# A decoder block on one core: residual rows loaded later, a small transposition moved ahead of a gate product, two value products set side by side

## The chip, the cores and the metric

The kernel runs on one core of a Trainium2 chip. The metric is the device time of one execution in microseconds (us). Before the change the median of three runs is 1652.53 us (1652.47 to 1653.07); the execution that the profiler recorded took 1651.61 us, of which its span covers 1649.8 us. The engines are named as in the profile: PE (matrix products; PEld is its weight load), DVE (vector), ACT (scalar and activation), POOL (GpSimd) and SP, which here only issues DMA transfers.

## The reference

One layer of a hybrid decoder block, 256 tokens, width 2048, float32 throughout. A combined input projection feeds two branches: gated linear attention (GLA, 4 heads) and forgetting attention (FoX, 8 heads). Both are projected to the model width, merged by sigmoid gates, sent through an output projection and added to the scaled residual before a layer norm. A gated MLP with a causal convolution (hidden width 5632), a second layer norm and a per-layer embedding follow.

```python
mix = token_mixers(x, w_in[i], w_gla_lr[i], b_gla_lr[i], gla_norm_g[i],
                   b_forget[i], w_branch_gla[i], w_branch_fox[i], w_out[i])
x = layer_norm(ALPHA * x + mix, ln1_g[i], ln1_b[i])
ffn = conv_gated_mlp(x, w_gate[i], w_up[i], conv_w[i], conv_b[i], w_down[i])
x = layer_norm(ALPHA * x + ffn, ln2_g[i], ln2_b[i])
x = x + jax.nn.sigmoid(x @ w_ple_gate[i]) * (p[i] @ w_ple_proj[i])
```

Within the FoX branch each head computes logits with a cumulative log-forget bias, a causal softmax in two blocks of 128 queries, and the product with the values:

```python
s = (jnp.einsum('bhqd,bhkd->bhqk', q_i, kh)
     + c_i[..., :, None] - c[..., None, :])
pr = jax.nn.softmax(s, axis=-1)
return jnp.einsum('bhqk,bhkd->bhqd', pr, vh)
```

## The kernel before, in words

All large products are split: each operand is written as a rounded part `hi` and a remainder `lo`, and hi·hi, hi·lo and lo·hi are summed in PSUM. A weight unit is 128 x 2048 numbers and comes as two raw rows `raw<unit>_0` and `raw<unit>_1` of 512 KB each. SP loads a raw row into one of four ring buffers, ACT rounds it to `hi` (L212), DVE subtracts to get `lo` (L217), and PE uses both. A ring buffer is free again when its `lo` is written, so a later raw row waits in SP's queue for a DVE instruction. Each engine works through its own queue in order, and SP's order is the program's own; on the other engines a scheduler sets the order by its estimate of when operands and buffers come free, except where the kernel pins it.

**The gates and the FoX heads.** Generators hold small work that is pulled in between the 128-column units of the q and k projections, one step after each unit. `gates_gen` computes the GLA decay of head h with two 96-row products (`psg`, L579); `fox_columns` (L565) transposes the forget sums `zc` into columns `ct` by two tiny PE instructions (`pct`). `fox_gen` handles the heads one behind the other: `turn(h)` transposes the softmax (`pt`, L645) and ACT copies it to `pts`; `values(h)` multiplies with the values (`po`, L652 and L654), after which ACT and DVE split the result.

**The output projection.** `residual("wo", ...)` calls `x_half` twice, once for each half of 1024 output columns. A half takes eight units 120 to 127 (second half: 128 to 135), called pairs 0 to 7 since each covers a pair of 128-row slices of the contraction; a unit's two raw rows belong to the two slices. Four PSUM banks `wo0_00`, `wo0_01`, `wo0_10`, `wo0_11` collect the half (first digit after the underscore: block of 128 tokens; second: block of 512 columns). In the first half, pairs 1, 2, 4 and 5 use a scheme with seven products instead of eight (`seven`, L354), with prepared sums `full` loaded from DRAM, and four more banks `wo0m0` to `wo0m3`; after pair 5 `joined` folds these four into the residual rows `z1` (DVE, `ju` and `z`, L1101 to L1111). After pair 7 the evacuation `ev` adds the four banks onto `z1` (L1090) and takes statistics (L1093). The second half needs four PSUM banks from the same pool of six: `wo1_00` and `wo1_01` take the place of `wo0m0` and `wo0m2`, `wo1_10` and `wo1_11` that of `wo0_00` and `wo0_01`, so that they are free once DVE's evacuation at L1090 has read these.

The `mid` dictionary of each half names callbacks that run after the work of a pair has been recorded: `mid1(t)` loads residual row block `z1[t]` (1 MB, on SP, L1172), `mid1g(i)` loads the layer norm's gain or offset, broadcast to 128 partitions (1 MB, on POOL's queue, `lnb`, L1138). Preparation runs up to three units ahead, so a callback after pair 2 stands in SP's queue behind the loads of pair 4.

## Time and profile before

| | before |
|---|---|
| median of three runs | 1652.53 us |
| profiled execution | 1651.61 us |
| its span | 1649.8 us |
| PE busy | 1643.6 us (100%) |
| DVE busy | 1233.6 us (75%) |
| ACT busy | 882.2 us (53%) |
| POOL busy | 94.8 us (6%) |

Times in the profile's views count from the start of the span. A timeline row gives the start, the duration, the engine, the source line, the operation, what it writes and reads, and how many were merged (x4); behind it in brackets how long the engine was idle before it, and what ended that. Consecutive PE instructions overlap: a row lasts longer than the distance to the next one's start, and it is this distance that a product costs.

### The profile page before, as it was taken

What the parts mean: (1) busy time and instruction counts of PE and PEld (TensorE: products, weight loads), DVE (VectorE), ACT (ScalarE), POOL (GpSimd) and SP (SyncE); (2) the same over time, 40 slices, a digit from 0 to 9 for tenths busy, and PEclk for the clock granted to TensorE, in tenths of its full rate; (3) what the DMA queues carried; (4) which work ended last, traced back from release to release, by engine and by line L of the source; (5) the groups of instructions that cost most, each with busy time, mean ns of one, the idle gap of its engine ahead of it and who ended that gap; (6) DMA issues with size and microseconds to landing.
All of it is one profiled execution on the core that took longest, in us unless ns stands there. A gap on an engine that the chain in (4) does not pass through costs nothing.

```text
span 1649.8 us, 24319 instructions
## 1 busy us (share of the span) xinstructions
PE 1643.6 (100%) x8956; PEld 1426.9 (86%) x8956; DVE 1233.6 (75%) x1819; ACT 882.2 (53%) x1268; POOL 94.8 (6%) x219
## 2 busy tenths in 40 slices
PE   9999999999999999999999999999999999999998
PEld 8988888888888888888888888888888888888887
DVE  6666658668856667786888778888887688788784
ACT  6745545445555455555565545555455566466643
POOL 0000000000000000000010011111110011010000
PEclk9999999999999999999999999999999999999999
DMA  7765555555555685668747678889886589799354
GB/s 299 233 196 189 168 186 178 183 179 179 174 180 195 242 307 192 193 206 316 267 155 234 232 257 334 316 325 337 322 285 229 192 292 325 270 329 363 141 187 170
DMA packets 107527, 394.23 MB, mean 239 GB/s; under 512 B 12504, under 2 KB 13408, under 8 KB 104464
## 3 DMA queue, kind: packets, MB, share of 16 engines
q1 hardware_dynamic: 97008, 352.62, 62.0%
q0 software_dynamic: 10256, 39.86, 6.3%
q8 instruction: 70, 1.15, 0.3%
q14 instruction: 49, 0.40, 0.1%
q10 hardware_dynamic: 144, 0.20, 0.0%
HBM read 365.36 MB, written 27.27 MB: 238 GB/s over the span
## 4 chain that ended last, share of the span: by engine, by line
PE 96%; DMA 2%; ACT 1%; DVE 1%; issue 0%; SPq 0%; ACTq 0%
PE psu L290 9%; PE psg L290 9%; PE dn L334 7%; PE psm L290 7%; PE gv L334 5%; PE gr L334 5%; PE pg L334 5%; PE psu L292 5%; PE psg L292 5%; PE psm L292 4%; PE psa L290 3%; PE wo L334 3%; PE dn L354 3%; PE fv L496 3%; PE dn0m L354 2%; PE psfq L290 2%
## 5 line engine op out<-in xcount | busy, mean ns | idle before, releaser
L217 DVE TENSOR_TENSOR lo<-raw,hi 128x1024 fp32r<-128x1024 f32 x502 | 611.5, 1224 | 271.9 <-ACT hi L212 270.3
L212 ACT ACTIVATE hi<-raw 128x1024 fp32r<-128x1024 f32 x502 | 528.7, 1059 | 465.4 <-DMA raw<-in_wu_dram 114.6
L290 PE MATMUL psu<-x1T,hi 128*128 128x512 f32 x688 | 236.0, 389 | 0.0
L290 PE MATMUL psg<-x1T,hi 128*128 128x512 f32 x672 | 230.5, 389 | 0.0
L292 PE MATMUL psu<-x1T,lo 128*128 128x256 f32 x688 | 189.9, 276 | 0.0
L292 PE MATMUL psg<-x1T,lo 128*128 128x256 f32 x672 | 185.5, 276 | 0.0
L290 PE MATMUL psm<-xT,hi 128*128 128x512 f32 x512 | 175.5, 390 | 0.0
L290 PEld LDWEIGHTS psu<-x1T,hi 128*128 128x128 f32 x688 | 129.1, 188 | 26.7
L290 PEld LDWEIGHTS psg<-x1T,hi 128*128 128x128 f32 x672 | 126.2, 188 | 26.1
L292 PE MATMUL psm<-xT,lo 128*128 128x256 f32 x512 | 141.4, 276 | 0.0
L292 PEld LDWEIGHTS psu<-x1T,lo 128*128 128x128 f32 x688 | 129.2, 188 | 0.0
L292 PEld LDWEIGHTS psg<-x1T,lo 128*128 128x128 f32 x672 | 126.1, 188 | 0.0
L290 PEld LDWEIGHTS psm<-xT,hi 128*128 128x128 f32 x512 | 96.1, 188 | 19.9
L334 PE MATMUL dn<-hi,hT 128*128 128x512 f32 x352 | 97.8, 389 | 0.0
L292 PEld LDWEIGHTS psm<-xT,lo 128*128 128x128 f32 x512 | 96.2, 188 | 0.2
L290 PE MATMUL psa<-oT,hi 128*128 128x512 f32 x256 | 87.8, 389 | 0.0
L334 PEld LDWEIGHTS dn<-hi,hT 128*128 128x128 f32 x352 | 66.0, 188 | 13.7
L292 PE MATMUL psa<-oT,lo 128*128 128x256 f32 x256 | 70.7, 276 | 0.0
L334 PE MATMUL gr<-hi,xT 128*128 128x512 f32 x256 | 70.6, 392 | 0.0
L334 PE MATMUL gv<-hi,xT 128*128 128x512 f32 x256 | 70.4, 391 | 0.0
L334 PE MATMUL pg<-hi,x2T 128*128 128x512 f32 (+1 forms) x224 | 60.0, 376 | 0.0
L290 PEld LDWEIGHTS psa<-oT,hi 128*128 128x128 f32 x256 | 48.1, 188 | 10.1
(357 smaller groups left out, 3070.4 us busy)
## 6 DMA issues: line engine op xcount, KB each, us to landing
raw<-in_wu_dram SPq DMA_DIRECT2D x528, 512.0 KB, 4.9
comb<-in_wu_dram SPq DMA_DIRECT2D x22, 768.0 KB, 8.9
tsd<-comb POOLq DMA_DIRECT2D x22, 512.0 KB, 7.3
top<-tsd SPq DMA_DIRECT2D x22, 512.0 KB, 5.8
fvraw<-in_wfv_dram SPq DMA_DIRECT2D x15, 524.0 KB, 7.9
rawf<-in_wu_dram SPq DMA_DIRECT2D x14, 512.0 KB, 9.5
top<-in_wu_dram SPq DMA_DIRECT2D x22, 256.0 KB, 6.8
hi<-hsd POOLq DMA_DIRECT2D x22, 256.0 KB, 4.9
```

The source lines that it names most:

```text
L212: c = nc.scalar.activation(hi, raw, AF.Copy, bias=0.0, scale=1.0)
L217: return nc.vector.tensor_tensor(lo, raw, hi.bitcast(F32), ALU.subtract)
L290: nc.tensor.matmul(ps, lhsT=hi[i // 8 if hoff == 0 else 0][:, w0 % 1024:w0 % 1024 + P], rhs=a[:, kt % 4, :], start=first and i == 0, stop= ...
L292: nc.tensor.matmul(ps[:, 256:512], lhsT=lo[i // 8 if hoff == 0 else 0][:, w0 % 1024:w0 % 1024 + P], rhs=a[:, kt % 4, 0:256], start=False, ...
L334: nc.tensor.matmul(bs[j][:, 0:m], lhsT=x, rhs=v[:, o:o + m], start=first and i == 0, stop=last and i == 2)
L354: nc.tensor.matmul(ps, lhsT=a, rhs=v, start=m and first and i == 0, stop=m and last and i == 2)
L496: nc.tensor.matmul(fbk[t][c][:, 0:n], lhsT=x, rhs=w[:, o:o + n], start=kt == 0 and i == 0, stop=kt == 15 and i == 2)
```

## The change

Three edits. The four callbacks of the output projection move: both residual row blocks are now loaded after pair 4 of the first half was recorded (before: after pairs 2 and 3), and the two affine rows after pairs 0 and 2 of the second half (before: after pair 6 of the first and pair 1 of the second). `fox_columns` runs just ahead of the gates of the last GLA head, in the same step, and not in a step of its own behind them. The values of the last FoX head follow those of the head before in the same step, and the loop loses its last round.

```diff
     def gates_gen():
         for h in range(H):
+            if h == H - 1:
+                fox_columns()
             gla_gates(h)
             yield
-        fox_columns()
...
-        for h in range(FH + 1):
-            if h < FH:
-                turn(h)
+        for h in range(FH):
+            turn(h)
             if h + 1 < FH:
                 logits(h + 1)
             if h > 0:
                 values(h - 1)
             if h + 1 < FH:
                 softmax(h + 1)
+            else:
+                values(h)
             yield
             yield
...
-    residual("wo", mT, 16, z1, st1, ({2: lambda: mid1(0), 3: lambda: mid1(1), 6: lambda: mid1g(0)}, {1: lambda: mid1g(1), 3: lambda: (pq.append(ple_prep(0)), mid1x())}), end=end1, ws=WOW)
+    residual("wo", mT, 16, z1, st1, ({4: lambda: (mid1(0), mid1(1))}, {0: lambda: mid1g(0), 2: lambda: mid1g(1), 3: lambda: (pq.append(ple_prep(0)), mid1x())}), end=end1, ws=WOW)
```

How this moves instructions is seen at three places. The first is SP's queue in the middle of the output projection's first half. `raw126` is pair 6, `raw127` pair 7, `raw128` the second half's first pair, `z10` and `z11` are the residual row blocks. Before:

```order
L149 DMA full124_7336<-tfd_105 128x2048
L1172 DMA z10_7247<-in_x_dram 128x2048
L147 DMA rawl125_7377<-in_wu_dram 128x512
L148 DMA raw125_7376<-in_wu_dram 128x1024
L149 DMA full125_7378<-tfd_105 128x2048
L1172 DMA z11_7248<-in_x_dram 128x2048
L205 DMA raw126_0_7421<-in_wu_dram 128x1024
L205 DMA raw126_1_7427<-in_wu_dram 128x1024
L205 DMA raw127_0_7454<-in_wu_dram 128x1024
L205 DMA raw127_1_7460<-in_wu_dram 128x1024
```

Now:

```order
L149 DMA full124_7336<-tfd_105 128x2048
L147 DMA rawl125_7376<-in_wu_dram 128x512
L148 DMA raw125_7375<-in_wu_dram 128x1024
L149 DMA full125_7377<-tfd_105 128x2048
L205 DMA raw126_0_7419<-in_wu_dram 128x1024
L205 DMA raw126_1_7425<-in_wu_dram 128x1024
L1174 DMA z10_7247<-in_x_dram 128x2048
L1174 DMA z11_7248<-in_x_dram 128x2048
L205 DMA raw127_0_7454<-in_wu_dram 128x1024
L205 DMA raw127_1_7460<-in_wu_dram 128x1024
```

Both 1 MB blocks moved behind pair 6's raw rows; pair 7's raw rows have the same transfers ahead of them as before. POOL's order, with the two affine rows, and what each of these two waits for are the same in both kernels.

The second place is PE at the start of the second half of the output projection. Before, the first 23 products of the half all go into `wo1_00` and `wo1_01`, from both slices of pairs 0 and 1, and only then comes the other token block, with the wait for its bank. The last three of the 23 and what follows:

```order
L334 MATMUL wo1_00_7579<-lo129_1_7544,mT0_5909 128x512 [waits DVE_49]
L334 MATMUL wo1_01_7580<-lo129_1_7544,mT0_5909 128x512
L334 MATMUL wo1_00_7579<-hi129_1_7543,mT0_5909 128x512
L334 MATMUL wo1_10_7581<-hi128_0_7499,mT0_5909 128x512 [waits DVE_49]
L334 MATMUL wo1_10_7581<-lo128_0_7500,mT0_5909 128x512
L334 MATMUL wo1_10_7581<-hi128_0_7499,mT0_5909 128x512
L334 MATMUL wo1_11_7582<-hi128_0_7499,mT0_5909 128x512 [waits DVE_49]
```

Now, from the half's first product on:

```order
L334 MATMUL wo1_00_7577<-hi128_0_7499,mT0_5909 128x512 [waits DVE_49,Activation_49]
L334 MATMUL wo1_01_7578<-hi128_0_7499,mT0_5909 128x512 [waits DVE_49]
L334 MATMUL wo1_00_7577<-lo128_0_7500,mT0_5909 128x512
L334 MATMUL wo1_01_7578<-lo128_0_7500,mT0_5909 128x512
L334 MATMUL wo1_00_7577<-hi128_0_7499,mT0_5909 128x512
L334 MATMUL wo1_01_7578<-hi128_0_7499,mT0_5909 128x512
L334 MATMUL wo1_10_7579<-hi128_0_7499,mT0_5909 128x512 [waits DVE_49]
L334 MATMUL wo1_11_7580<-hi128_0_7499,mT0_5909 128x512 [waits DVE_49]
```

The first use of `wo1_10` has moved from the 24th place of the half to the 7th. In both kernels it waits for the same DVE instruction, the evacuation of `wo0_00` (L1090 before, L1092 now), and `wo1_11` for that of `wo0_01`; DVE's own order there is the same in both: the `lo` of pair 7, then `joined` mixed with the `lo` of units 128 and 129, then the evacuation.

The third place is PE where the last FoX head is turned. Before:

```order
L292 MATMUL psk0_2067<-xT3_109,lo24_1_1942 128x256
L645 MATMUL pt7_2103<-ident_82,lg_1990 128x128 [waits DVE_49,Activation_49]
L645 MATMUL pt7_2103<-ident_82,lg_1990 128x128 x2
L652 MATMUL po6_2109<-pts_1985,fv_120 128x256
L654 MATMUL po6_2109<-pts_1985,fv_120 128x128
L290 MATMUL psk1_2126<-xT0_106,hi25_0_2009 128x512
```

Now:

```order
L292 MATMUL psk0_2067<-xT3_109,lo24_1_1942 128x256
L646 MATMUL pt7_2103<-ident_82,lg_1990 128x128 [waits DVE_49,Activation_49]
L646 MATMUL pt7_2103<-ident_82,lg_1990 128x128 x2
L653 MATMUL po6_2109<-pts_1985,fv_120 128x256
L655 MATMUL po6_2109<-pts_1985,fv_120 128x128
L653 MATMUL po7_2114<-pts_2107,fv_120 128x256 [waits Activation_49]
L655 MATMUL po7_2114<-pts_2107,fv_120 128x128
L290 MATMUL psk1_2131<-xT0_106,hi25_0_2009 128x512
```

`po7` reads `pts_2107`, ACT's copy of `pt7`. Before, it stood 64 products (two units) further on, behind the units `psk1` and `psk2`; now two products lie between `pt7` and it. The small transposition `pct` also moved on PE, from its place one unit behind the last gate product `psg` to directly ahead of it.

## The prediction

> **What bounds the kernel now.** I read the page's engine line first, then PE's waits, then the timelines of the places where the edits fall.

> ```profile
> PE 1643.6 (100%) x8956; PEld 1426.9 (86%) x8956; DVE 1233.6 (75%) x1819; ACT 882.2 (53%) x1268; POOL 94.8 (6%) x219
> PE warm_ps L128 <- DVE warm L125: 1.2, 1, 1.2
> PE wo L334 <- DVE lo L217: 0.2, 1, 0.2
> PE ptl L1056 <- DVE x1T L878: 0.2, 1, 0.2
> ```

> PE is never out of work: in 1649.8 us it waits twice after the start, for 0.2 us each. So no transfer and no other engine can give more than tenths of a microsecond back, while anything that makes PE wait is paid in full. One of the two waits, in the output projection (`wo`), lies where the residual loads move.

> **The loads: what can be gained.** SP's queue, the DMA issues of the stretch 761 to 766 us against those of the whole run, ACT, and PE around pair 6:

> ```profile
> 755.97 0.42 SPq L1172 DMA_DIRECT2D z<-in_x_dram  x1
> 760.46 0.43 SPq L1172 DMA_DIRECT2D z<-in_x_dram  x1
> raw<-in_wu_dram SPq DMA_DIRECT2D x2, 512.0 KB, 17.2
> raw<-in_wu_dram SPq DMA_DIRECT2D x528, 512.0 KB, 4.9
> 777.44 1.06 ACT L212 ACTIVATE hi<-raw 128x1024 fp32r<-128x1024 f32 x1 [5.75 <-DMA raw<-in_wu_dram]
> 780.20 1.06 ACT L212 ACTIVATE hi<-raw 128x1024 fp32r<-128x1024 f32 x1 [1.70 <-DMA raw<-in_wu_dram]
> 778.96 0.84 PE L334 MATMUL wo<-hi,mT 128*128 128x512 f32 x3
> 782.57 0.73 PE L334 MATMUL wo<-lo,mT 128*128 128x512 f32 x2 [0.21 <-DVE lo L217]
> 789.96 1.07 PE L334 MATMUL wo<-hi,mT 128*128 128x512 f32 x4
> 791.32 0.39 PE L334 MATMUL wo<-hi,mT 128*128 128x512 f32 x1
> ```

> Pair 6's raw rows, queued behind both residual blocks, take 17.2 us to land where 4.9 is usual; the second reaches ACT at 780.20 and PE has to wait for its `lo`. From 789.96 to 791.32 PE issues four products and two of the next row: 1.36 / 6 = 0.227 us each, the undisturbed rate. Pair 6 starts at 778.96; the first two of the four at 789.96 end pair 7, so 46 products lie between, which would take 10.43 us and took 11.00. The wait with its surroundings costs **0.57 us**. With the blocks behind pair 6's rows, 2 MB fewer stand ahead of these, 5 us at the 415 GB/s below; they land several microseconds sooner and the 0.57 is gained: the second half then starts at 790.41 (two products after 789.96) less 0.57, **789.84**.

> **The loads: what is late next.** The second half's seventh product, now the first on `wo1_10`, waits for DVE's evacuation of `wo0_00`. DVE in this stretch (rows left out are more of `joined` and `lo`), and PE where this product stood before:

> ```profile
> 778.53 1.23 DVE L217 TENSOR_TENSOR lo<-raw,hi 128x1024 fp32r<-128x1024 f32 x1 [5.40 <-ACT hi L212]
> 781.29 3.67 DVE L217 TENSOR_TENSOR lo<-raw,hi 128x1024 fp32r<-128x1024 f32 x3 [1.54 <-ACT hi L212]
> 784.88 0.68 DVE L1106 TENSOR_TENSOR ju<-ju,wo0m 128x512 f32<-128x512 f32 x1
> 785.48 0.68 DVE L1111 SCALAR_TENSOR_TENSOR z<-z,wo0m 128x512 f32<-128x512 f32 x1
> ...
> 790.56 1.23 DVE L217 TENSOR_TENSOR lo<-raw,hi 128x1024 fp32r<-128x1024 f32 x1 [0.33 <-ACT hi L212]
> ...
> 793.50 1.22 DVE L217 TENSOR_TENSOR lo<-raw,hi 128x1024 fp32r<-128x1024 f32 x1
> 794.64 1.28 DVE L1090 TENSOR_TENSOR z<-z,wo 128x512 f32<-128x512 f32 x2
> 795.41 0.62 PE L334 MATMUL wo<-hi,mT 128*128 128x512 f32 x2
> ```

> The evacuation starts at 794.64; one such operation takes 0.68 (row at 784.88) and the next starts 0.60 later, so `wo0_00` is free at 795.32 and `wo0_01` at 795.92. Before, PE got there with its 24th product, the second of the row at 795.41, at 795.64: 0.3 us after the bank was free, with nothing lost. Now it gets there at 789.84 + 6 x 0.227 = **791.20**.

> Can DVE be sooner? Twelve instructions stand between the `lo` of pair 7 and the evacuation, and DVE works through them in 9.8 us (784.88 to 794.64) with one gap of 0.33. They begin when pair 7's second `lo` is written, which hangs on this landing:

> ```profile
> 782.65 1.06 ACT L212 ACTIVATE hi<-raw 128x1024 fp32r<-128x1024 f32 x1 [0.18 <-DMA raw<-in_wu_dram]
> 755.00:760.00 5.00, 5.00 (x24) 4.14 (x23) 5.00 (x8) 2.60 (x5) 0.00 (x0) 1.00 0.73 224
> 760.00:765.00 5.00, 5.00 (x24) 4.14 (x23) 2.97 (x4) 2.83 (x3) 0.00 (x0) 1.00 1.01 415
> 775.00:780.00 5.00, 5.00 (x24) 4.02 (x23) 1.23 (x1) 1.06 (x1) 0.00 (x0) 1.00 1.00 413
> ```

> ACT's rounding of that row waits for the DMA until 782.65. From 760 to 780 the DMA engines are full (shares 1.01 and 1.00 in the first and last of four windows). Pair 7's rows keep the same bytes ahead of them as before, the two affine rows on POOL's queue included, so reordering what is ahead does not let them land sooner. They might land later, if taking the block issued at 755.97 out of the not yet full stretch (0.73) leaves the engines idle; the `full` load issued just ahead of it, at 1 MB, has 2.5 us of work for them, so I expect little, up to 1 us. What can fall away is the gap of 0.33 before 790.56, where DVE waits, by way of ACT, for a raw row of the second half: with pair 6 done early, the rows ahead of that one are issued sooner and it shares the DMA engines with fewer.

> From DVE's end to PE's start it takes 0.05: the first `lo` of the row at 781.29, 1.23 long, ends at 782.52, and PE, which waited for it, goes on at 782.57. So PE has the bank between 795.0 and 795.4. PE waits 3.75 to 4.2 us at `wo1_10`, issues one product, and waits 0.60 - 0.23 = 0.37 more at `wo1_11`: 4.1 to 4.55 lost. Behind the waiting product stands everything PE has left to do. Less the 0.57, the edit costs **3.5 to 4.0; I take 3.85**, nearer the end with DVE unchanged, because a restart after a wait costs some 0.1 too (the row at 782.57: 0.73 for two where 0.62 is usual). With pair 7 later by 1 us it is 4.9; with the banks freed 1 us sooner 2.8. Nothing later gives it back, since PE finds no other wait to shorten but 0.2 at `ptl`. The affine rows keep their place and their releasers on POOL: 0.

> **The values.** PE and ACT where the last head is turned:

> ```profile
> 202.94 0.60 PE L652 MATMUL po<-pts,fv 128*128 128x256 f32 x2
> 203.37 0.38 PE L654 MATMUL po<-pts,fv 128*128 128x128 f32 x2
> 203.51 0.47 PE L290 MATMUL psk<-xT,hi 128*128 128x512 f32 x1
> 202.74 1.06 ACT L212 ACTIVATE hi<-raw 128x1024 fp32r<-128x1024 f32 x1 [1.66 <-PE psk L290]
> 203.97 0.48 ACT L116 ACTIVATE pts<-pt 128x384 f32<-128x384 f32 x1
> ```

> `po7` now follows `po6` and could issue at about 203.50. It needs `pts`, which ACT writes from 203.97 to 204.45, because a rounding of 1.06 us that itself waited for PE stands first in its queue. Before, two units of other products covered this copy; the cover is gone. PE waits 204.45 + 0.05 - 203.50 = **1.0 us**, and behind it waits the whole unit `psk1`. Bounds: +0.9 if the two seams between `po` and `psk` become one (0.47 on the first `psk` where 0.40 is usual), +1.2 with the 0.1 of a restart. I take 1.0.

> **The transposition.** PE around it:

> ```profile
> 80.42 0.28 PE L292 MATMUL psfq<-xT,lo 128*128 128x256 f32 x1
> 80.62 0.28 PE L565 MATMUL pct<-ident,zc 8*128 8x8 f32 x2
> 80.84 0.50 PE L290 MATMUL psfq<-xT,hi 128*128 128x512 f32 x1
> 81.18 0.28 PE L292 MATMUL psfq<-xT,lo 128*128 128x256 f32 x1
> 61.12 0.28 DVE L560 COPY zc<-zf 8x256 f32<-8x256 f32 x1
> ```

> The interlude takes 81.18 - 80.42 = 0.76 us; the two `psfq` products alone take 0.34 (0.227 for 512 columns, half of it for 256), so it costs 0.42. Its operand `zc` is ready at 61.40, long before. Next to the gate product it has one seam with `psfq` in place of two: it saves 0.2 at best (half of it), and costs 0.1 more at worst if its seam with `psg` is as dear. I take **-0.05**.

> **The sum.** 3.85 + 1.0 - 0.05 = **+4.8 us**: 1651.61 becomes 1656.4 in a profiled execution. The median was 0.92 above the profiled one; the same on top gives **1657.3**. By the terms' own bounds (2.8 to 4.9, 0.9 to 1.2, -0.2 to +0.1) the likeliest case reaches from +3.5 to +6.2, most of it +4.0 to +5.6.

> **The rivals.** (1) *The array's clock drops in the long wait.* The last window of the run shows the granted clock (the column after POOL's) falling when PE stops:

> ```profile
> 1645.00:1650.00 5.00, 0.49 (x5) 0.29 (x3) 1.32 (x4) 0.38 (x1) 0.00 (x0) 0.92 0.29 105
> 1.20 3.25 PE L128 MATMUL warm_ps<-warm 128*128 128x512 bf16 x8 [1.20 <-DVE warm L125]
> ```

> PE ends at 1645.49; a mean of 0.92 with half speed at the end means 0.8 us of it, so the drop came at 1649.2, 3.7 us later. The wait here is 3.75 to 4.2. Were the clock halved for 3.7 us behind it, PE would lose 1.85 of them: +6.65, 1659.2. At the start of the run eight products took 3.25 us, 0.41 each against 0.227, so half speed does occur on a PE that comes from idleness. Against it: the array still works on the last product after its issue (0.39 against a distance of 0.227), and the reaction is seen once, at one phase. [...] Chance 0.10.

> (2) *The bank is free sooner.* If pair 7's rows land 2 us sooner, because the DMA engines move the new order faster, `joined` starts sooner too and the loss at `wo1_10` shrinks to 1.85: the sum is +2.8, 1655.3. For it: DVE stood idle for 5.40 us ahead of 778.53 and would have time for pair 6 there; against it the full DMA windows. Chance 0.13.

> (3) *Not slower.* The same mechanism pushed to its end: the evacuation must be done by 791.2 at the first use, 4.1 us sooner. Only then does the edit gain its 0.57, and the sum is -0.57 + 1.0 - 0.05 = +0.4, 1652.9, no change that can be told. It needs pair 7's rows in at about 778.5, 1.7 MB earlier in a full queue. Chance 0.08.

> (4) *Pair 7's rows are late.* They stand directly behind both blocks now. Landing 1.5 us later would move the evacuation with them and make it +6.3, 1658.8. Chance 0.07.

> That leaves 0.62 for the forecast. A measurement of this kernel tells 0.2%, 3.3 us, from no change, so slower begins at 1655.8. Slower: the forecast, (1), (4) and a little of (2): 0.82; same 0.16; faster 0.02. The range that leaves out about 2 in 10 is 1655.0 to 1659.4.

> **What would show it.** In PE's waits of the changed kernel two new rows: one at `wo` for DVE's `z` (the evacuation) of about 4 us in the second half's first pair, with a second of 0.4, and one at `po` for ACT's `pts` of about 1 us; the old row at `wo` for `lo` gone. ACT's rounding of pair 6 should start some 8 us sooner, that of pair 7's second row near 782.7 on a clock that is set back by the 1.0 from the values. The forecast is wrong if DVE's evacuation starts near 791, if `po7` issues without a wait, or if a window behind the long wait shows a clock below 1.

## The result, and the profile after

The changed kernel takes 1658.66 us, median of 6 runs (1657.33 to 1659.93), against 1652.38 us of the kernel before (6 runs, 1651.65 to 1653.07): the ratio is 1.0038 with a 95% interval of 1.0026 to 1.0049, so it is 6.3 us slower. 1657.3 was predicted, with a range of 1655.0 to 1659.4. The profiled execution is the quickest of the six, 1657.33 us with a span of 1655.6.

The engine line of the changed kernel's profile page:

```profile
PE 1646.2 (99%) x8956; PEld 1428.2 (86%) x8956; DVE 1232.6 (74%) x1819; ACT 881.9 (53%) x1268; POOL 96.4 (6%) x219
```

And two rows of its PE waits (engine, line, what it waited for: us in total, times, longest):

```profile
PE wo L334 <- DVE z L1092: 2.1, 1, 2.1
PE po L653 <- ACT pts L116: 0.7, 1, 0.7
```

Both forecast waits are there, each shorter in these rows than the 4 and 1 us forecast, and the old wait at `wo` for `lo` is gone. PE's timeline of the changed kernel around the long wait, with DVE's evacuation that ends it:

```profile
792.49 0.61 PE L334 MATMUL wo<-hi,mT 128*128 128x512 f32 x2
795.22 1.18 PE L334 MATMUL wo<-hi,mT 128*128 128x512 f32 x2 [2.12 <-DVE z L1092]
796.20 1.05 PE L334 MATMUL wo<-lo,mT 128*128 128x512 f32 x2
797.05 1.91 PE L334 MATMUL wo<-hi,mT 128*128 128x512 f32 x4
794.49 1.27 DVE L1092 TENSOR_TENSOR z<-z,wo 128x512 f32<-128x512 f32 x2
```

Without the wait the first product on `wo1_10` would have issued at 792.49 + 2 x 0.227 = 792.94; it issues at 795.22, so **2.28 us** are lost. The last PE row shows something else: four products in 1.91 us where the row of the kernel before has 1.07. The stretches of the changed kernel, cut where the clock changes (length, then busy time of PE, PEld, DVE, ACT and POOL with instruction counts, then the granted clock, the DMA share and GB/s):

```profile
789.27:792.69 3.42, 3.42 (x16) 2.82 (x16) 3.42 (x5) 1.06 (x1) 0.00 (x0) 1.00 0.81 228
792.69:796.10 3.41, 1.19 (x4) 0.47 (x3) 3.41 (x6) 2.11 (x2) 0.00 (x0) 1.00 0.77 257
796.10:799.51 3.41, 3.41 (x9) 2.65 (x9) 3.41 (x7) 1.06 (x1) 0.00 (x0) 0.50 0.40 139
799.51:802.93 3.42, 3.42 (x16) 2.79 (x16) 3.42 (x4) 1.07 (x1) 0.00 (x0) 1.00 0.35 108
```

**The clock was halved for 3.41 us behind the wait**: 9 products were busy there where the stretches around it have 16, some 1.6 us lost. So the first rival came true although the wait was shorter than the one it had been given a chance of 0.10 for.

The values, PE and ACT of the changed kernel:

```profile
203.32 0.38 PE L655 MATMUL po<-pts,fv 128*128 128x128 f32 x2
204.45 0.70 PE L653 MATMUL po<-pts,fv 128*128 128x256 f32 x2 [0.75 <-ACT pts L116]
205.13 0.47 PE L290 MATMUL psk<-xT,hi 128*128 128x512 f32 x1
202.69 1.06 ACT L212 ACTIVATE hi<-raw 128x1024 fp32r<-128x1024 f32 x1 [1.66 <-PE psk L290]
203.92 0.48 ACT L116 ACTIVATE pts<-pt 128x384 f32<-128x384 f32 x1
```

The bracket counts the idle time from the end of `po6`. By starts it is more: in the kernel before, the next product follows 0.14 us behind the start of such a row (203.37 and 203.51), so `po7` could have issued at 203.46 and did at 204.45, **0.99 us** later.

Where the time went, by the first product of each stage (after less before, one profile each): 0.45 us more before the first `psfq` unit, in waits of `fv` at the start that no edit touches; -0.50 from there to the first `psq`, where the transposition lies; **+1.79** between the first `psk` and `gv` (values); **+3.80** between the first `wo` and `pp` (residual); in the 800 us behind it -0.2 and, in the last stage, +0.4. Tempting as it is, this is no proof of what each edit costs: the experiments show that two of the four numbers depend on other things.

### The profile page after: what moved, and what is told of

Its sections match the earlier page's. It is cut to its first block, busy times and chain, and to the rows that moved or that the text cites. A ratio compares the mean times of both kernels' runs of the same rounds, so it can differ in the third digit from the quotient of the medians.

```text
span 1655.6 us, 24318 instructions
## 1 busy us (share of the span) xinstructions
PE 1646.2 (99%) x8956; PEld 1428.2 (86%) x8956; DVE 1232.6 (74%) x1819; ACT 881.9 (53%) x1268; POOL 96.4 (6%) x219
## 4 chain that ended last, share of the span: by engine, by line
PE 95%; DMA 2%; DVE 1%; ACT 1%; issue 0%; SPq 0%; ACTq 0%; DVEq 0%
PE psu L290 9%; PE psg L290 9%; PE dn L334 7%; PE psm L290 7%; PE gv L334 5%; PE gr L334 5%; PE pg L334 5%; PE psu L292 5%; PE psg L292 5%; PE psm L292 4%; PE psa L290 3%; PE dn L354 3%; PE wo L334 3%; PE fv L496 3%; PE dn0m L354 2%; PE psk L290 2%
## 5 line engine op out<-in xcount | busy, mean ns | idle before, releaser
L217 DVE TENSOR_TENSOR lo<-raw,hi 128x1024 fp32r<-128x1024 f32 x502 | 610.7, 1222 | 284.5 <-ACT hi L212 283.1
L212 ACT ACTIVATE hi<-raw 128x1024 fp32r<-128x1024 f32 x502 | 528.5, 1059 | 474.2 <-DMA raw<-in_wu_dram 110.3
L290 PE MATMUL psu<-x1T,hi 128*128 128x512 f32 x688 | 236.0, 389 | 0.0
L290 PE MATMUL psg<-x1T,hi 128*128 128x512 f32 x672 | 230.5, 389 | 0.0
L292 PE MATMUL psu<-x1T,lo 128*128 128x256 f32 x688 | 189.9, 276 | 0.0
L292 PE MATMUL psg<-x1T,lo 128*128 128x256 f32 x672 | 185.5, 276 | 0.0
L290 PE MATMUL psm<-xT,hi 128*128 128x512 f32 x512 | 175.5, 390 | 0.0
L290 PEld LDWEIGHTS psu<-x1T,hi 128*128 128x128 f32 x688 | 129.2, 188 | 26.7
L290 PEld LDWEIGHTS psg<-x1T,hi 128*128 128x128 f32 x672 | 126.1, 188 | 26.2
L292 PE MATMUL psm<-xT,lo 128*128 128x256 f32 x512 | 141.4, 276 | 0.0
L292 PEld LDWEIGHTS psu<-x1T,lo 128*128 128x128 f32 x688 | 129.1, 188 | 0.0
L292 PEld LDWEIGHTS psg<-x1T,lo 128*128 128x128 f32 x672 | 126.2, 188 | 0.0
L290 PEld LDWEIGHTS psm<-xT,hi 128*128 128x128 f32 x512 | 96.1, 188 | 19.8
L334 PE MATMUL dn<-hi,hT 128*128 128x512 f32 x352 | 97.8, 389 | 0.0
L292 PEld LDWEIGHTS psm<-xT,lo 128*128 128x128 f32 x512 | 96.2, 188 | 0.2
L290 PE MATMUL psa<-oT,hi 128*128 128x512 f32 x256 | 87.8, 389 | 0.0
L334 PEld LDWEIGHTS dn<-hi,hT 128*128 128x128 f32 x352 | 66.0, 188 | 13.7
L292 PE MATMUL psa<-oT,lo 128*128 128x256 f32 x256 | 70.7, 276 | 0.0
L334 PE MATMUL gr<-hi,xT 128*128 128x512 f32 x256 | 70.6, 392 | 0.0
L334 PE MATMUL gv<-hi,xT 128*128 128x512 f32 x256 | 70.3, 391 | 0.0
L334 PE MATMUL pg<-hi,x2T 128*128 128x512 f32 (+1 forms) x224 | 60.0, 376 | 0.0
L334 PE MATMUL wo<-hi,mT 128*128 128x512 f32 x192 | 54.6, 396 | 2.2 <-DVE z L1092 2.1
## 6 DMA issues: line engine op xcount, KB each, us to landing
raw<-in_wu_dram SPq DMA_DIRECT2D x528, 512.0 KB, 4.9
tsd<-comb POOLq DMA_DIRECT2D x22, 512.0 KB, 7.4
top<-tsd SPq DMA_DIRECT2D x22, 512.0 KB, 5.6
rawf<-in_wu_dram SPq DMA_DIRECT2D x14, 512.0 KB, 9.9
```

What stands on the lines that cost most here:

```text
L212: c = nc.scalar.activation(hi, raw, AF.Copy, bias=0.0, scale=1.0)
L217: return nc.vector.tensor_tensor(lo, raw, hi.bitcast(F32), ALU.subtract)
L290: nc.tensor.matmul(ps, lhsT=hi[i // 8 if hoff == 0 else 0][:, w0 % 1024:w0 % 1024 + P], rhs=a[:, kt % 4, :], start=first and i == 0, stop= ...
L292: nc.tensor.matmul(ps[:, 256:512], lhsT=lo[i // 8 if hoff == 0 else 0][:, w0 % 1024:w0 % 1024 + P], rhs=a[:, kt % 4, 0:256], start=False, ...
L334: nc.tensor.matmul(bs[j][:, 0:m], lhsT=x, rhs=v[:, o:o + m], start=first and i == 0, stop=last and i == 2)
```

## The experiments

"Before" is timed on the same chip beside each group (medians 1652.38 for e1 to e4, 1652.33 for e5 to e8, 1652.92 for e9 to e12). The last column is the time from the first product of `wo` to the first of `pp` in the run's profile; the kernel before has 85.29, the changed one 89.10.

| run | what | median us | ratio to before (95%) | `wo` to `pp` |
|---|---|---|---|---|
| e1 | residual part | 1658.64 | 1.0037 (1.0023 to 1.0050) | 91.57 |
| e2 | residual part, products in the old order | 1652.59 | 1.0001 (0.9992 to 1.0010) | 85.57 |
| e3 | transposition part | 1651.94 | 0.9997 (0.9989 to 1.0006) | 85.59 |
| e4 | values part | 1654.71 | 1.0015 (1.0006 to 1.0023) | 84.74 |
| e5 | e1, affine rows late | 1652.35 | 0.9999 (0.9990 to 1.0008) | 84.97 |
| e6 | before, affine rows late | 1652.14 | 0.9997 (0.9988 to 1.0006) | 84.71 |
| e7 | e1, six products more ahead of the wait | 1657.10 | 1.0027 (1.0018 to 1.0036) | 87.19 |
| e8 | whole change, products in the old order | 1653.75 | 1.0007 (0.9998 to 1.0016) | 84.71 |
| e9 | residual blocks alone | 1657.68 | 1.0032 (1.0019 to 1.0044) | 91.66 |
| e10 | values one unit behind | 1652.44 | 0.9999 (0.9990 to 1.0008) | 85.31 |
| e11 | e3, e6 and e10 together | 1651.89 | 0.9995 (0.9986 to 1.0004) | 84.71 |
| e12 | whole change again | 1657.88 | 1.0035 (1.0022 to 1.0048) | 88.48 |

**e1, the residual part alone** (from the kernel before):

```diff
-({2: lambda: mid1(0), 3: lambda: mid1(1), 6: lambda: mid1g(0)}, {1: lambda: mid1g(1), 3: lambda: (pq.append(ple_prep(0)), mid1x())})
+({4: lambda: (mid1(0), mid1(1))}, {0: lambda: mid1g(0), 2: lambda: mid1g(1), 3: lambda: (pq.append(ple_prep(0)), mid1x())})
```

> Only the residual's part of the change: both blocks behind pair 6's raw rows, the affine rows in the second half; transposition and values stay as before. In the changed kernel PE loses 3.80 us between the start of the second half of the output projection and its end. If that part acts alone: 3.5 to 4.1 us slower than before, a wait of about 2 us at `wo` for DVE's `z`, and 3.4 us of halved clock behind it. If the loss needed the other two edits as well (the shift of 1.74 us that they bring before this place sets the wait against the clock's windows in another way): no halved clock, and 1.8 to 2.4 us slower.

It loses 6.26 us, as much as the whole change and more than either expectation. Its row of PE's waits:

```profile
PE wo L334 <- DVE z L1090: 3.7, 1, 3.7
```

Its PE and DVE timelines at that place:

```profile
791.55 0.61 PE L334 MATMUL wo<-hi,mT 128*128 128x512 f32 x2
795.84 1.39 PE L334 MATMUL wo<-hi,mT 128*128 128x512 f32 x2 [3.68 <-DVE z L1090]
795.10 1.28 DVE L1090 TENSOR_TENSOR z<-z,wo 128x512 f32<-128x512 f32 x2
```

And its stretches between changes of the clock, with the columns of above:

```profile
791.54:794.96 3.42, 0.62 (x3) 0.19 (x1) 3.42 (x5) 1.06 (x1) 0.00 (x0) 1.00 0.79 252
794.96:798.37 3.41, 2.53 (x6) 1.83 (x7) 3.41 (x7) 1.06 (x1) 0.00 (x0) 0.50 0.67 217
798.37:801.79 3.42, 3.42 (x10) 2.64 (x9) 3.42 (x5) 1.06 (x1) 0.00 (x0) 0.50 0.04 16
801.79:805.20 3.41, 3.41 (x16) 2.79 (x15) 2.55 (x3) 1.06 (x1) 0.00 (x0) 1.00 0.69 220
```

The wait is 795.84 - 792.00 = 3.84 us, what had been forecast for the whole change, and the clock is halved for twice 3.41 us: in the first of these PE still waits at the start and is busy for 2.53 us, and only after the second, in which PE never stopped (3.42 of 3.42 us), is the clock full again. Lost at half speed: some 14 products at 0.2 us each, 2.8. With the floor of 84.71 in the table's last column, 84.71 + 3.84 + 0.37 + 2.8 = 91.7, and 91.57 was measured.

**e2, the same loads with the products in the old order:**

```diff
-                mm(i, unit(), (0, 1))
+                w = unit()
+                if name == "wo1" and i < 2:
+                    us = [w] if i == 0 else us + [w]
+                    mm(i, w, (0,))
+                    if i == 1:
+                        mm(0, us[0], (1,))
+                        mm(1, us[1], (1,))
+                else:
+                    mm(i, w, (0, 1))
```

> The residual's part again, with the products of the second half's pairs 0 and 1 written so that those on token block 0 of both pairs come first, as they stood before; DMA issues and evacuations are those of e1. If the loss comes from the order of the products alone: `wo1_10` is reached some 24 products after the half starts, 3.9 us later than in e1, by then the bank is free, the waits for `z` and for pair 6's `lo` are both gone, and it is 0.3 to 0.6 us faster than before. If the loss comes from the loads (rows of pair 7 or of the second half landing later): 1 us or more slower, with a wait at `wo` for DVE's `lo` or `z`.

The six microseconds are gone: the loss comes from the order of the products that the moved loads brought about. The expected gain of 0.3 to 0.6 did not come either, and one row of PE's timeline of this run shows where it went:

```profile
796.29 0.74 PE L334 MATMUL wo<-lo,mT 128*128 128x512 f32 x2 [0.52 <-DVE lo L217]
```

DVE works without a gap from 786 to 797 us on `joined`, `lo` and evacuations; the wait at pair 6 has moved to the second half.

**e3, the transposition part, and e4, the values part**, each alone:

```diff
+            if h == H - 1:
+                fox_columns()
             gla_gates(h)
             yield
-        fox_columns()
```

```diff
-        for h in range(FH + 1):
+        for h in range(FH):
...
             if h + 1 < FH:
                 softmax(h + 1)
+            else:
+                values(h)
```

> Only the transposition's part of the change. By the forecast's price (one seam less): 0.05 us faster, between 0.2 faster and 0.1 slower. By the pace theory (PE goes through pairs of unit products at 0.341 or 0.352 us each, and what small product stood last before them decides which): the 70 slow pairs behind the transposition become fast, 0.5 to 0.8 us faster, and the trace shows no slow stretch between 76 and 105 us.

> Only the values' part of the change. By the wait for ACT's copy of `pts` alone: 1.0 us slower (0.9 to 1.2). With the pace theory: 0.7 us of wait, some 0.3 us of seams, and about 80 pairs of unit products behind it at 0.352 in place of 0.341 us, another 0.8: 1.6 to 2.0 us slower, with one slow stretch from 205 to 243 us.

e3's 0.44 us cannot be told from nothing. The `L290` products of the same 22 us behind the transposition in the kernel before (length, PE busy with the count, PEld, clock, DMA share, GB/s):

```profile
82.00:104.00 22.00, 22.00 (x64) 11.79 (x64) 1.00 0.57 190
```

The same stretch of e3 has two more:

```profile
82.00:104.00 22.00, 22.00 (x66) 12.15 (x65) 1.00 0.58 193
```

But so has e1, which does not touch this place:

```profile
82.00:104.00 22.00, 22.00 (x66) 12.18 (x65) 1.00 0.58 193
```

There are two paces, one pair (`hi` and `lo`) each about 0.350 us or each about 0.340 us, and e1 has the quick one without the edit, as have seven of the nine profiles without it. So the -0.50 in the comparison above is not the edit's doing, and my pace theory of e3 falls. What the edit is worth shows among the profiles with the quick pace: from the first `psfq` to the first `psfk` these seven take 45.11 or 45.12 us, and e3, e8, e11 and e12, which have the edit, 45.07 or 45.08. That is 0.04 us less, as forecast. (The changed kernel has 45.20, with a slower first unit ahead of the edit.)

e4 is 2.33 us slower by the medians (by the interval 1.0 to 3.8). In its profile 1.94 us are lost between `psk` and `gv`: the joined group takes 1.10 more than the two apart (2.24 us beyond `pt7` and the products around it, against twice 0.57), and 1.0 of it is the late issue of `po7`. The rest is pace, seen again in a count of `L290` products from 217 to 240 us, here in the kernel before:

```profile
217.00:240.00 23.00, 23.00 (x69) 12.74 (x68) 1.00 0.59 188
```

In e4 there are two fewer:

```profile
217.00:240.00 23.00, 23.00 (x67) 12.39 (x66) 1.00 0.58 190
```

The second profile of the whole change (e12) has as many as before:

```profile
217.00:240.00 23.00, 23.00 (x69) 12.68 (x68) 1.00 0.59 193
```

Behind the joined group the slow pace held in three of four profiles that have it (e4, e8, the changed kernel) and not in e12; behind a `po7` of its own the pace was quick in all profiles (ten). 80 pairs by 0.010 are the missing 0.8 us. What sets the pace is open.

**e5 and e6, the affine rows late on SP's queue**, on top of e1 and of the kernel before (e5's table of loads is that of e1; e6 keeps the blocks at 2 and 3):

```diff
-        q = nc.gpsimd if li == 0 else nc.sync
+        q = nc.sync
```

```diff
-({2: lambda: mid1(0), 3: lambda: mid1(1), 6: lambda: mid1g(0)}, {1: lambda: mid1g(1), 3: lambda: (pq.append(ple_prep(0)), mid1x())})
+({2: lambda: mid1(0), 3: lambda: mid1(1)}, {0: lambda: mid1g(0), 2: lambda: mid1g(1), 3: lambda: (pq.append(ple_prep(0)), mid1x())})
```

> e1 with one change: the two affine rows (1 MB each) go onto SP's queue behind raw rows of the second half, so they no longer share the DMA engines with pair 7's raw rows; the order of the products is that of e1 (`wo1_10` at the seventh place). If DVE's evacuation of `wo0_00` hangs on the bytes ahead of pair 7's second row, that row lands up to 5 us sooner (2 MB at 413 GB/s), the evacuation starts some 4 us sooner, and the wait of 3.7 us at `wo` for `z` with the halved clock is gone: between 0.6 us faster than before and 0.6 slower. If the evacuation is bound by DVE's own work or by when the rows are issued: 4 us or more slower, as in e1.

> The kernel before with that change alone (affine rows on SP's queue in the second half); residual blocks and the order of the products stay as before. Pair 6's rows then share with 2 MB less: the wait of 0.2 us at `wo` for `lo` goes or stays, between 0.6 us faster and no change. If the rows on SP's queue hold up raw rows of the second half: up to 1 us slower, with a wait at `wo` for `lo` near 800 us.

In e5 the order is e1's and the wait is gone. ACT's rounding of pair 7's two rows and DVE's evacuation in e5:

```profile
778.12 1.06 ACT L212 ACTIVATE hi<-raw 128x1024 fp32r<-128x1024 f32 x1 [6.56 <-DMA raw<-in_wu_dram]
779.33 1.06 ACT L212 ACTIVATE hi<-raw 128x1024 fp32r<-128x1024 f32 x1
790.90 1.28 DVE L1090 TENSOR_TENSOR z<-z,wo 128x512 f32<-128x512 f32 x2
```

The same two roundings in e1:

```profile
782.32 1.06 ACT L212 ACTIVATE hi<-raw 128x1024 fp32r<-128x1024 f32 x1 [10.64 <-DMA raw<-in_wu_dram]
783.53 1.06 ACT L212 ACTIVATE hi<-raw 128x1024 fp32r<-128x1024 f32 x1 [0.15 <-DMA raw<-in_wu_dram]
```

Row and evacuation are both 4.2 us sooner, for 2 MB taken out of full DMA engines (in e1 their share is 1.00 to 1.02 from 765 to 780 us): the evacuation does hang on the bytes ahead of pair 7's second row. With that, 0.57 was to be gained, and the profiles show 0.32 and 0.58 of it (84.97 and 84.71 in the last column where the kernel before has 85.29); the timed runs cannot tell it from nothing.

**e7, six products more ahead of the wait:**

```diff
+                if name == "wo1" and i < 1:
+                    mm(i, w, (0,))
+                    mm(i, w, (1,))
```

> e1 with the products of the second half's pair 0 written with all twelve on token block 0 first, so that `wo1_10` is reached six products, 1.36 us, later: a wait of about 2.4 us in place of 3.7. If a wait of that length already halves the clock for 3.4 us (as in the changed kernel, where PE waited 2.1 us): 3.5 to 4.5 us slower than before. If the clock needs an idle stretch as long as its window: no halved clock, 2.0 to 2.6 us slower.

Its median is 4.8 us slower, beyond both expectations, and its eleven times spread from 1653.11 to 1659.91: in the quickest the mean granted clock is 1.000, in four of the others 0.998. Its profile is of an execution in which the clock stayed full. The row of PE's waits:

```profile
PE wo L334 <- DVE z L1095: 1.8, 1, 1.8
```

The two stretches that hold the wait:

```profile
791.12:794.53 3.41, 2.71 (x12) 1.90 (x11) 3.41 (x5) 1.70 (x2) 0.00 (x0) 1.00 0.80 231
794.53:797.94 3.41, 2.21 (x8) 1.61 (x9) 3.41 (x7) 1.31 (x2) 0.00 (x0) 1.00 0.76 251
```

The wait lies across a boundary of the clock's 3.41 us stretches (counted back in steps of 3.413 us from the clock's drop at the end of the run, since it does not change here), and PE is busy 2.71 and 2.21 us in the two. So it also matters how the wait lies in these stretches, as e12 below shows: its wait, across a boundary as well, is longer than the changed kernel's, 3.27 us against 2.28, and leaves the clock full. The size of the median is not explained by this one profile.

**e8, the whole change with the products in e2's order** (its diff is e2's, on the changed kernel):

> The whole change, with the order of products of e2 in the second half (no early `wo1_10`). If the parts only seemed not to add up because the values' delay is swallowed by the long wait at `wo`, then without that wait it shows in full: +2.3 (values) + 0.2 (e2) - 0.4 (transposition), about 2.1 us slower than before. If the values' part costs little once the transposition has moved too: 0 to 1 us slower.

1.42 us slower by the medians, between the two expectations; the interval, 0.9998 to 1.0016, just reaches no change. No wait is left at `wo`. In the profile the values cost 1.78 us (`psk` to `gv`); the stage from `wo` to `pp` is 0.86 shorter than in e2, whose code is the same there. So in these two profiles part of the values' delay is made up in that stage even without the long wait; whether by PE's later arrival or by how the loads happened to land is not shown.

**e9, the residual blocks alone, and e12, the whole change again:**

```diff
-({2: lambda: mid1(0), 3: lambda: mid1(1), 6: lambda: mid1g(0)}, {1: lambda: mid1g(1), 3: lambda: (pq.append(ple_prep(0)), mid1x())})
+({4: lambda: (mid1(0), mid1(1)), 6: lambda: mid1g(0)}, {1: lambda: mid1g(1), 3: lambda: (pq.append(ple_prep(0)), mid1x())})
```

> Half of the residual's part: only the two residual blocks go behind pair 6's raw rows, the affine rows' loads stay where they were written before. The order of the products comes out as in e1 (`wo1_10` seventh). If the blocks' place alone makes that order and the long wait: 5.5 to 6.5 us slower, as e1, with a wait of 2 to 4 us at `wo` for `z` and a halved clock. If the affine rows' place takes part: 1 us or more apart from e1.

> The whole change once more, beside e9 on one chip, for a second profile. If the values' delay (about 1.8 us) is swallowed by the wait at `wo`: its median lies within 0.7 us of e9's, its wait at `wo` for `z` is 1.4 to 2 us shorter than e9's, and the joined values are followed by the slow pace up to the next group. If the wait does not depend on when PE arrives: about 2 us slower than e9.

The blocks alone make the order and the loss. e9 is 4.76 us slower, less than expected and 1.5 less than e1; but the whole change, too, is 4.96 slower here and 6.28 in its first runs, and `wo` to `pp` takes as long in e9 as in e1 (91.66 and 91.57), so this does not speak for a part of the affine rows. And the whole change is 0.2 us from e9, though the values alone cost 2.33: by the medians of five runs each, which spread over 3 to 4 us, the values add nothing. The two profiles do not show how. e9 waits 4.0 us and e12 3.27, but PE arrives at the wait at the same time in both (the last product before it starts at 792.22 and 792.18), and the pace behind e12's joined values was the quick one, so that they cost it only 0.68 us (`psk` to `gv`). The shorter wait comes from an evacuation that starts 0.79 sooner, at 794.94 against 795.73. The row of e12's PE waits:

```profile
PE wo L334 <- DVE z L1092: 3.1, 1, 3.1
```

In e12's profile a boundary cuts the wait in two, and the clock stays full:

```profile
790.87:794.28 3.41, 1.70 (x8) 1.08 (x6) 3.41 (x6) 1.87 (x2) 0.00 (x0) 1.00 0.74 238
794.28:797.69 3.41, 1.92 (x7) 1.39 (x8) 3.41 (x6) 1.06 (x1) 0.00 (x0) 1.00 0.68 247
```

This execution is the quickest of its five, 1656.43 us; two of the other four have a clock of 0.997, two of 0.998.

**e10, the last values one unit behind, and e11, the three small edits:**

```diff
             yield
+            if h + 1 == FH:
+                values(h)
             yield
```

> The values' part with `values(7)` one unit of other products behind `values(6)`, neither joined to it (as in the change) nor two units behind it (as before). If the loss of e4 is the wait for ACT's copy plus the slow pace that follows the joined group: no wait at `po`, slow pace for 15 pairs at most, then fast, and the time of before within 0.3 us. If any earlier place of the last values costs: 1 us or more slower.

> The kernel before with the transposition ahead of the gate product (e3), the affine rows late on SP's queue (e6) and the last values one unit behind (e10). If the gains of e3 and e6 are real and add: 0.6 us faster than before, 0.4 to 1.2, which this measurement can hardly tell from none; the trace would show no wait at `wo` and no slow pace between 76 and 105 us. If they were chance: within 0.3 us of before.

e10 has no wait at `po`, one unit covers the copy; it is 0.5 us faster by the medians, which its interval does not tell from no change. e11 is 1.0 us faster than before by the medians, the quickest kernel here; its interval, 0.9986 to 1.0004, does not exclude no change. Its profile has no wait at `wo` or `po`.

## Why the prediction came out as it did

**Loads, the gain of 0.57: right as the price of the old wait.** Five profiles without a wait in the stage have 84.71 to 84.97 us, four of them up to 84.74, where the kernel before has 85.29. The edit does take it out of the first half: in e1 the second half starts 40.82 us behind the first product of `wo` (six products ahead of 792.00), before 41.39. But e2, with the long wait gone, has a new wait of 0.52 in the second half and 85.57 in all, so nothing of the gain is left there.

**Loads, the wait at `wo1_10`: right in place and cause, and to a tenth in size, for the edit alone.** Forecast were an arrival at 791.20 and a free bank between 795.0 and 795.4. In e1, whose `wo` starts 0.80 later, they are 792.00 and 795.84, that is 791.20 and 795.04. e2 shows that the order is the cause, e5 that the bytes ahead of pair 7 are what the evacuation hangs on. The 0.37 at `wo1_11` came as forecast.

**The clock: the step that failed, in the sum's residual term.** The chance of 0.10 was my estimate, for a clock that halves only after a whole stretch without PE work. No run shows such a need: in the changed kernel PE was busy for 1.19 of the 3.41 us, and the clock halved all the same. In e1 it stayed halved for 6.8 us, not 3.7, which costs 2.8 in place of the rival's 1.85. The residual part alone is +6.26 where 3.85 was forecast. The wait in e1's profile was sized right, so the term that was too small is the clock's, put at nothing in the sum.

**The values: the wait right, the pace behind it left out, and the sum not additive.** `po7` issued 0.99 us late where 1.0 was forecast, and the joined group with its seams costs 1.10, inside the 0.9 to 1.2 given. The slow pace behind it, +0.8 in e4, was no term of the sum. The prediction then added the values' delay to the wait at `wo1_10`, which means that DVE's evacuation is set back as far as PE is ("on a clock that is set back by the 1.0 from the values"). In the changed kernel's profile it is not: it started at 794.49, where 794.64 set back by 1.0 had been expected. ACT and SP of the kernel before, at the second `full` block:

```profile
751.30 1.06 ACT L116 ACTIVATE ts<-full 128x1024 fp32r<-128x1024 f32 x1 [3.96 <-DMA full<-tfd]
755.12 0.33 SPq L148 DMA_DIRECT2D raw<-in_wu_dram  x1
```

The same two rows of the changed kernel, which issues this block at the same distance from PE:

```profile
750.48 1.06 ACT L116 ACTIVATE ts<-full 128x1024 fp32r<-128x1024 f32 x1 [1.40 <-DMA full<-tfd]
754.29 0.33 SPq L148 DMA_DIRECT2D raw<-in_wu_dram  x1
```

PE is 1.74 us later there and SP issues the block as much later, but it landed in 4.9 us in place of 7.5 and was in 0.8 us sooner; the later issues follow it. With the values' delay alone (e4), or in the whole change with the old order (e8), the evacuation did move back. Its rows in e4 and e8:

```profile
797.21 1.28 DVE L1091 TENSOR_TENSOR z<-z,wo 128x512 f32<-128x512 f32 x2
796.62 1.27 DVE L1100 TENSOR_TENSOR z<-z,wo 128x512 f32<-128x512 f32 x2
```

PE reaches `wo` 3.12 and 2.82 us later there than in the kernel before, and the evacuation starts 2.57 and 1.98 later. So in these two it follows PE for the most part. The rest goes with how quickly the block lands: in the eleven profiles with the affine rows on POOL's queue the evacuation starts 43.74 us behind the first product of `wo` where the block took 4.9 us, 44.7 to 45.3 where it took 6.2 to 6.5, and 45.5 to 45.9 where it took 6.9 to 7.9. The four profiles with joined values have 4.9 to 6.4, but e6 without them has 4.9 and e1 6.2. Why the block lands so differently, and whether the values' delay has a part in it, is open; one profile gives the wait only to about 1.5 us.

So why the medians show no addition is explained only in part: by the shorter waits (2.28 and 3.27 where e1 and e9 have 3.84 and 4.0) and by fewer halved stretches (one and none, against two each). Of these, e12's profile is of its quickest execution and e9's of its slowest.

**The transposition: right that it is next to nothing;** e3's interval reaches from -1.8 to +1.0 us, and the profiles at the quick pace give -0.04 where -0.05 was forecast.

**The sum.** +4.8 was forecast and +6.28 measured, inside the range. Its make-up differs: the residual part alone costs as much, with the clock's share missing from my term, and the values, 2.33 by themselves, add nothing on top. Two errors of opposite sign, 2.4 too little and 1.0 too much, left one of 1.5. That they cancelled so far is luck.

**What would show it:** ACT rounded pair 6 at 768.74 and 771.38, 8.7 us sooner, as forecast, and pair 7's second row at 782.92 (forecast: near 782.7, set back by 1.0):

```profile
768.74 1.04 ACT L212 ACTIVATE hi<-raw 128x1024 fp32r<-128x1024 f32 x1
771.38 1.06 ACT L212 ACTIVATE hi<-raw 128x1024 fp32r<-128x1024 f32 x1 [1.60 <-PE wo L334]
782.92 1.06 ACT L212 ACTIVATE hi<-raw 128x1024 fp32r<-128x1024 f32 x1 [0.17 <-DMA raw<-in_wu_dram]
```

The window behind the wait shows a clock below 1, which had been named as what would make the forecast wrong.

## What to carry to other kernels

When loads move, look first at what the scheduler then does with the instructions that use them: here the order of a few products cost six microseconds, and the moved bytes themselves nothing that could be measured. A PE wait of two to four us, as here, has to be costed with the clock behind it: 2.28 us of wait were followed by 3.41 us at half speed in the changed kernel, 3.84 us by 6.8 in e1, and 3.27 us by none in e12, where the wait lies across two of the clock's stretches. And two costs on one path need not add: measure them together as well as apart, and take more than one profile where the wait hangs on a landing.

## What the runs showed of the hardware

```profile
1646.62:1650.04 3.42, 1.35 (x12) 1.14 (x10) 2.18 (x5) 0.72 (x2) 0.00 (x0) 1.00 0.31 115
1650.04:1652.30 2.26, 0.00 (x0) 0.00 (x0) 0.00 (x0) 0.00 (x0) 0.00 (x0) 0.50 0.17 58
```

The same in e10:

```profile
1644.52:1647.93 3.41, 1.67 (x14) 1.47 (x13) 2.46 (x6) 0.77 (x2) 0.00 (x0) 1.00 0.31 115
1647.93:1650.50 2.57, 0.00 (x0) 0.00 (x0) 0.00 (x0) 0.00 (x0) 0.00 (x0) 1.00 0.15 51
```

So in the stretches given here half speed came after 1.35 us of PE's busy time or less, and full speed stayed after 1.67 us or more.

Pairs of products of 512 and 256 columns went through PE at about 0.340 or 0.350 us at a granted clock of 1.00 and with PE busy for 22.00 of 22.00 us in both (e1 and the kernel before, 82 to 104 us), and kept the pace over up to 112 pairs (changed kernel, 205.13 to 244.29 us) until a group of other products came between. With the same kernel the pace behind one group differed: behind the joined values it was 0.350 us in the first profile of the whole change and 0.340 in e12 (67 and 69 `L290` products from 217 to 240 us).
